# A fused low-rank update on one Trainium2 core: five loads and four stores in place of ten and eight

## The chip, the cores and the metric

The kernel runs on one core of one Trainium2 chip. The metric is device time in microseconds (us). Each time below is the median of the runs made of that kernel; the runs of one kernel lie within about one per cent of their median. A profile is taken of one of these runs and shows its span, 1.6 to 1.9 us shorter than the time. Times inside a run are counted from the start of the profile's span.

## The reference

```python
x: (16, 512, 768) float32;  A: (768, 16);  B: (16, 768);  scale = 0.5
out = x + scale * ((x @ A) @ B)
```

The 8192 rows of x and of the result are 25.2 MB each way. A and B are 48 KB each.

## The kernel before

Partition p holds 64 consecutive rows of x, so a load of n "rows" moves n x 3 KB of contiguous memory into each of 128 partitions. Everything is loaded into one buffer, changed in place, and stored from it. These are the parts that matter:

```python
LOAD_ROWS = [1, 3, 4] + [8] * 7          # rows of each load, per partition
STORE_ROWS = [8] * 8                     # rows of each store

a_f32 = const.tile([P, ND, R], fp32, name="a_f32")
nc.scalar.dma_start(out=a_f32, in_=A.rearrange("(c p) r -> p c r", p=P))     # ScalarE's queue
r = 0
for n in LOAD_ROWS:
    nc.sync.dma_start(out=x_all[:, ds(r, n), :], in_=xv[:, ds(r, n), :])     # SyncE's queue
    r += n
# [cut]
b_f32 = const.tile([R, D], fp32, name="b_f32")
nc.scalar.dma_start(out=b_f32, in_=B)
# [cut: casts of A and B to float16, the identity]

# for each step of up to 4 rows:
#   transposed(): 6 x 4 TensorE transposes of x, copied to SBUF by ScalarE
#   down():       6 matmuls with A into yt, scaled by VectorE
#   up_and_add(): for the step before: 2 matmuls with B, added to the row by VectorE
#   finished():   issues a store on SyncE's queue as soon as all of its rows are done
```

A is read with its 16-element rows spread over partitions and chunks, so its load consists of 768 pieces of 64 bytes, 48 for each of the 16 DMA engines. An x load has 128 pieces, 8 for each engine, one per partition (128 packets for each load).

## Time and profile before

| | before |
|---|---|
| time | 125.2 us |
| span of the profiled run | 123.6 us |
| x queue (q1), share of the 16 engines' span | 96.0% |
| TensorE busy | 80% |
| A landed | 4.7 us |
| last store issued / last packet written | 107.8 / 122.0 us |

The page of the kernel before, parts 1 and 2. The 40 digits are equal slices of the span, each the busy share in tenths.

```profile
PE 98.4 (80%) x614; PEld 60.9 (49%) x614; DVE 68.7 (56%) x83; ACT 52.4 (42%) x103; POOL 0.7 (1%) x6
...
PE   0569997999999999999999999999999995300000
...
DMA  4999999999999999999999999999999999999981
```

The DMA engines are full from the second slice to near the end. The queue table and the list of issues (the last column is the time from issue to landing):

```profile
q1 hardware_dynamic: 2592, 50.33, 96.0%
q10 hardware_dynamic: 816, 0.10, 0.6%
...
out_dram<-x_all SPq DMA_DIRECT2D x8, 3072.0 KB, 28.6
x_all<-in_x_dram SPq DMA_DIRECT2D x7, 3072.0 KB, 37.5
...
a_f_77<-in_A_dram ACTq DMA_DIRECT2D x1, 48.0 KB, 3.9
```

q1 is SyncE's queue with x and the result; q10 is ScalarE's, with A and B.

The kernel is bound by DMA: 25 MB in, then 25 MB out, with nothing between.

### The profile page before, as it was taken

The page shows a single profiled execution, that of the slowest core. Times are in us where ns is not written, and L with a number is a line of the kernel's source. Part 1 is how long each engine was busy: PE and PEld are TensorE (multiplying, and loading weights), DVE is VectorE, ACT ScalarE, POOL GpSimd, SP SyncE. Part 2 cuts the span into 40 slices and gives each one's busy share as a digit, 9 for nine tenths or more (in the row PEclk, how much of TensorE's full clock was granted, in tenths as well). Part 3 has the DMA queues.
Part 4 walks back from the last instruction along what each step waited for, and adds up shares of the span by engine and source line. Part 5 has one row for each costly group of instructions (what it writes and reads, how often), then busy time and mean ns, then how long its engine had stood idle before and what let it go on. Part 6 is the DMA issues. An engine that isn't in the chain of part 4 may idle for free.

```text
span 123.6 us, 1623 instructions
## 1 busy us (share of the span) xinstructions
PE 98.4 (80%) x614; PEld 60.9 (49%) x614; DVE 68.7 (56%) x83; ACT 52.4 (42%) x103; POOL 0.7 (1%) x6
## 2 busy tenths in 40 slices
PE   0569997999999999999999999999999995300000
PEld 0356472847575666666665747475656662000000
DVE  0023156666857677686868686867576688900000
ACT  4315363547373737365555546373737360000000
POOL 2000000000000000000000000000000000000000
PEclk9999999999999999999999999999999999855555
DMA  4999999999999999999999999999999999999981
GB/s 72 383 409 442 477 414 398 485 379 453 430 390 496 398 411 453 406 469 406 406 475 392 446 422 430 453 406 435 430 422 461 392 453 427 414 469 398 446 366 48
DMA packets 3416, 50.54 MB, mean 409 GB/s; under 512 B 1088, under 2 KB 1088, under 8 KB 1232
## 3 DMA queue, kind: packets, MB, share of 16 engines
q1 hardware_dynamic: 2592, 50.33, 96.0%
q10 hardware_dynamic: 816, 0.10, 0.6%
q8 instruction: 5, 0.08, 0.3%
q14 instruction: 3, 0.02, 0.0%
HBM read 25.26 MB, written 25.17 MB: 408 GB/s over the span
## 4 chain that ended last, share of the span: by engine, by line
PE 75%; DMA 5%; DVE 4%; issue 1%; DVEq 1%; SPq 0%
PE xt_ps L82 39%; PE lora_ps L108 19%; PE yt_ps L92 17%; DMA x_all<-in_x_dram 5%; DVE x_all L112 3%; DVE yt_sb L96 1%; DVEq L177 1%; SPq L60 0%
## 5 line engine op out<-in xcount | busy, mean ns | idle before, releaser
L112 DVE TENSOR_TENSOR x_all<-x_all,lora_ps 128x768 f32<-128x768 f32 x64 | 58.3, 951 | 28.7 <-PE lora_ps L108 28.7
L84 ACT CAST xt_sb<-xt_ps 128x512 f16<-128x512 f32 (+2 forms) x102 | 51.2, 568 | 47.3 <-PE xt_ps L82 47.1
L82 PE MATMUL xt_ps<-ident,x_all 128*128 128x128 f32 x384 | 52.0, 287 | 5.6 <-DMA x_all<-in_x_dram 5.6
L82 PEld LDWEIGHTS xt_ps<-ident,x_all 128*128 128x128 f32 x384 | 43.4, 145 | 17.9 <-issue 10.6
L108 PE MATMUL lora_ps<-b_mm,yt_sb 16*128 16x512 f16 (+1 forms) x128 | 27.0, 326 | 2.7 <-DVE yt_sb L96 1.6
L92 PE MATMUL yt_ps<-xt_sb,a_mm 128*16 128x512 f16 (+2 forms) x102 | 24.8, 384 | 0.0
L108 PEld LDWEIGHTS <-yt_sb 16*128 16x128 f16 x128 | 9.4, 93 | 13.8 <-issue 6.8
L92 PEld LDWEIGHTS <-a_mm 128*16 128x16 f16 x102 | 8.0, 93 | 13.6 <-issue 6.0
L96 DVE TENSOR_SCALAR yt_sb<-yt_ps 16x512 f16<-16x512 f32 (+2 forms) x17 | 10.9, 641 | 3.6 <-PE yt_ps L92 3.6
L72 DVE CAST a_mm<-a_f_77 128x96 f16<-128x96 f32 x1 | 0.2, 209 | 4.7 <-DMA a_f_77<-in_A_dram 4.7
L84 ACT ACT_TABLE_LOAD x1 | 1.3, 1283 | 1.8 <-issue 1.8
L74 DVE CAST b_mm<-b_f_89 16x768 f16<-16x768 f32 x1 | 0.5, 548 | 2.1 <-DMA b_f_89<-in_B_dram 2.1
masks.py:199 POOL TENSOR_SCALAR_AFFINE_SELECT ident<-ident 128x128 f32<-128x128 f32 x1 | 0.3, 292 | 0.1
masks.py:197 POOL MEMSET ident<- 128x128 f32 x1 | 0.2, 204 | 0.3 <-POOLq L163 0.3
L163 POOL MEMSET const-bfloat16-1.0<- 128x1 bf16 x1 | 0.1, 102 | 0.0
L163 POOL MEMSET const-uint8-127<- 128x1 uint8 x1 | 0.1, 102 | 0.0
L163 POOL MEMSET const-float32-0.0<- 128x1 f32 x1 | 0.1, 98 | 0.2 <-issue 0.2
L163 POOL MEMSET const-float32-1.0<- 128x1 f32 x1 | 0.1, 98 | 0.0
## 6 DMA issues: line engine op xcount, KB each, us to landing
out_dram<-x_all SPq DMA_DIRECT2D x8, 3072.0 KB, 28.6
x_all<-in_x_dram SPq DMA_DIRECT2D x7, 3072.0 KB, 37.5
x_all<-in_x_dram SPq DMA_DIRECT2D x1, 1536.0 KB, 10.0
x_all<-in_x_dram SPq DMA_DIRECT2D x1, 1152.0 KB, 6.7
x_all<-in_x_dram SPq DMA_DIRECT2D x1, 384.0 KB, 3.6
a_f_77<-in_A_dram ACTq DMA_DIRECT2D x1, 48.0 KB, 3.9
b_f_89<-in_B_dram ACTq DMA_DIRECT2D x1, 48.0 KB, 5.8
```

The lines of the kernel that those rows point to most:

```text
L72: nc.vector.tensor_copy(out=a_mm, in_=a_f32)
L74: nc.vector.tensor_copy(out=b_mm, in_=b_f32)
L82: nc.tensor.transpose(xt_ps[:, s, :], row(r0 + s)[:, ds(j * P, P)], ident)
L84: nc.scalar.copy(out=xt_sb[:, 0 : S * P], in_=xt_ps[:, 0:S, :])
L92: nc.tensor.matmul(yt_ps[:, 0:n], a_mm[:, j, :], xt[:, 0:n], start=(j == 0), stop=(j == ND - 1))
L96: nc.vector.tensor_scalar(out=yt_sb[:, 0:n], in0=yt_ps[:, 0:n], scalar1=sc, scalar2=None, op0=mybir.AluOpType.mult,)
L108: nc.tensor.matmul(lora_ps[:, ds(n0, n)], yt_sb[:, ds(s * P, P)], b_mm[:, ds(n0, n)], start=True, stop=True,)
L112: nc.vector.tensor_tensor(out=row(r0 + s), in0=row(r0 + s), in1=lora_ps, op=mybir.AluOpType.add)
L163: nc = _bacc.Bacc("TRN2", target_bir_lowering=False, num_devices=1)
L177: with _tile.TileContext(nc) as tc:
```

## The change

The intent: larger transfers, fewer of them, less fixed cost.

```diff
-LOAD_ROWS = [1, 3, 4] + [8] * 7
-STORE_ROWS = [8] * 8
+LOAD_ROWS = [4, 12, 16, 16, 16]
+STORE_ROWS = [20, 20, 16, 8]
```

Nothing else changes.

## The prediction

> **What bounds the kernel now.** The DMA queue. The page's queue table gives q1 96.0% of the 16 engines' span; the table of windows, 425 to 430 GB/s in every 10 to 20 us stretch from 20 to 120 us. All loads are queued ahead of the stores. TensorE heads the chain of waits (75%), but by the timeline the last store is issued at 107.84 us and lands 14.6 us later, because the store before it occupies the engines until 112.7 (first engine) to 114.8 us (last one), by its completion packets. TensorE has 4 to 6 us of slack.

> **Removed.** Per-packet cost. The DMA packet records give minima of 121 ns for 3 KB, 347 for 9 KB, 460 for 12 KB, 912 for 24 KB: 27.2 B/ns plus about 8 ns per packet. Data packets fall from 144 to 72 per engine: 72 x 8 ns = 0.58 us, and nine completion packets of 9 ns: -0.66 us. Nothing else in the 118.6 us of queue work shrinks.[...]

> **Moved.** Rows become usable later.
> - The first four rows land at about 7.8 us as before (the 3-row load released TensorE at 8.0), but the 1-row start at 4.5 us is gone.
> - Step 0 (24 transposes at the cold 213 ns, six matmuls) runs from 8.0 to 14 or 16 us. Rows 4 to 7 now come with a 12-row load; the first 16 rows land at about 18.8 us. Before, that step started at 15.05. TensorE idles 3 to 5 us.
> - That should drop the clock again. [...] The trace agrees: transposes are 213 ns apart before 15.2 us and 109 after, and the granted clock falls to 0.5 at 107.4 us after a sparse stretch. [...]
> - From the start of the rows-4-to-7 step to the last store's issue took 92.8 us; one more row of up-projection falls in it (+0.4). The last store is issued at about 18.9 + 92.8 + 0.4[...] = 114.6 us (112 without re-cooling), just past the drain of the stores ahead of it, now 112 to 114 us. Its first packet follows 1.05 us after issue (as for the first load), its eight packets per engine take 7.3 us: last packet at 123.0, against 122.06 before.

> Later loads (32 rows by 33.5 us, needed at 36) and the other stores (ready well before their turn) don't bind.

> **Prediction.** The 0.66 us gained is eaten by a late last store: 125.9 us, +0.6%. Without re-cooling 124.6; with a slow re-warm 127. Range 124.4 to 127.3. Faster by over 2%: 2%; within 2%: 90%; slower: 8%.

> **What would show it.** 1296 packets on q1; 48 KB packets near 1.81 us, 60 KB near 2.27. A TensorE wait of 3 to 5 us for a load, ending near 19 us[...]. Last store issued at 113 to 116 us, with a dip in DMA share just after 112, landing about 9 us after issue instead of 14.6.

> **What would make it wrong.** Long packets split or slower per byte; the clock staying warm (then 124.6); engines drifting further apart behind longer packets; larger first packets delaying A past 13 us.

The sum for the last store's issue came to 114.6 us; the term for re-warming is cut out of it, and the three that stand come to 112.1. The totals with re-cooling (125.9, and 127 with a slow re-warm) rest on that term, which was the author's estimate and was not shown.

## More of the kernel before

A landed 3.9 us after its issue at 0.7 us. The waits of all engines (engine, line, what it waited for: us in total, times, longest):

```profile
PE xt_ps L82 <- DMA x_all<-in_x_dram: 5.6, 2, 4.5
DVE a_mm L72 <- DMA a_f_77<-in_A_dram: 4.7, 1, 4.7
```

TensorE is held up by data for only 5.6 us, at the start.

## The result, and the profile after

| | before | after |
|---|---|---|
| time | 125.18 us | 181.68 us |
| span | 123.6 | 179.8 |
| x queue, share of the engines' span | 96.0% | 65.4% |
| A landed | 4.7 us | 62.5 us |
| last store issued | 107.8 us | 164.1 us |

The ratio is 1.451, 95% interval 1.446 to 1.457. A ratio here is the mean time of one kernel's fast runs over that of the other's fast runs of the same rounds, so it is not quite the ratio of the medians quoted.

The same parts of the page after the change:

```profile
PE 99.2 (55%) x608; PEld 62.2 (35%) x608; DVE 68.4 (38%) x82; ACT 51.8 (29%) x97; POOL 0.7 (0%) x6
...
PE   0440000000000095999899999999999999961000
...
DMA  6999898989898400000000599950099990898892
```

TensorE does the same work, but stands still for eleven slices, about 50 us. The DMA engines stand still as well, later: the loads are through at slice 14, and no row is ready to be stored until slice 23. The queue table and issues:

```profile
q1 hardware_dynamic: 1296, 50.33, 65.4%
q10 hardware_dynamic: 816, 0.10, 0.4%
...
a_f_77<-in_A_dram ACTq DMA_DIRECT2D x1, 48.0 KB, 61.7
b_f_84<-in_B_dram ACTq DMA_DIRECT2D x1, 48.0 KB, 61.4
```

The x queue itself did what was hoped: half the packets, and 65.4% of 179.8 us is 117.6 us of work against 118.7 before. But A, 48 KB, took 61.7 us to land instead of 3.9. The waits:

```profile
DVE a_mm L72 <- DMA a_f_77<-in_A_dram: 62.5, 1, 62.5
PEld L92 <- DVE a_mm L72: 52.3, 1, 52.3
PE yt_ps L92 <- DVE a_mm L72: 51.9, 1, 51.9
...
PE xt_ps L82 <- DMA x_all<-in_x_dram: 7.1, 1, 7.1
```

Read this as a chain: VectorE's cast of A waits for A's DMA until 62.5 us, and the first matmul that uses A (L92) waits 51.9 us for that cast. x itself was waited for only once, for the first load. The chain of waits on the page names this stretch "another core or an unknown queue 34%"; the list of waits is the view that names A.

The table of windows shows what the delay costs the DMA queue (columns: window, length, busy time of TensorE's matmuls, its weight loads, VectorE, ScalarE and GpSimd with counts, granted clock, DMA share, GB/s). First two windows of the kernel before, then three of the changed one:

```profile
15.00:60.00 45.00, 44.23 (x293) 28.14 (x292) 31.08 (x37) 24.11 (x47) 0.00 (x0) 1.00 1.00 429
65.00:100.00 35.00, 35.00 (x232) 21.89 (x231) 25.48 (x32) 18.76 (x36) 0.00 (x0) 1.00 1.00 429
```

```profile
15.00:60.00 45.00, 0.00 (x0) 0.00 (x0) 0.00 (x0) 0.00 (x0) 0.00 (x0) 1.00 1.01 433
65.00:100.00 35.00, 32.34 (x192) 20.10 (x192) 20.02 (x24) 16.32 (x31) 0.00 (x0) 0.95 0.00 1
120.00:130.00 10.00, 10.00 (x64) 5.86 (x62) 7.60 (x9) 5.43 (x11) 0.00 (x0) 1.00 0.01 2
```

Before, both work all the time. After, from 15 to 60 us only DMA works, from 65 to 100 us only the compute engines. Two stages that overlapped now follow each other. The third line is the wait for the second 20-row store.

Why was A late? The trace records each DMA packet with its queue, size and time. Each load and store of x also leaves 16 packets of 4 bytes (288 for 18 transfers before, 144 for nine after), which start as its data packets end; they are the completion packets, read here as one per engine. Counting the data packets that start in each 0.2 us (this is a tabulation of those records, not a view of the page):

```
            x packets started      A packets started
before
3.3 us      23 of 3 KB              58
3.5          4 of 3 KB, 1 of 9 KB  300
3.7          1 of 3 KB, 7 of 9 KB  308
3.9          9 of 9 KB              82
4.1         11 of 9 KB              20
after
4.1          5 of 12 KB              5
4.3          9 of 12 KB              9
4.5          5 of 12 KB              5
7.5          8 of 36 KB              8
7.7          6 of 36 KB              6
7.9          2 of 36 KB              2
```

In these counts after the change, one 64-byte piece of A passes for each x packet, whether that packet is 12 or 36 KB. Over the whole load phase 41 of A's 48 pieces per engine passed, beside 37 x packets (the few extra pieces passed where one x load ended and the next began); the last seven went when the x queue was empty. In the kernel before, A's pieces ran almost alone: the single-row first load was nearly over when they arrived at 3.35 us, and no packet of the second load started before 3.70 us.

### The profile page after: what moved, and what is told of

Its sections match the earlier page's. It is cut to its first block, busy times and chain, and to the rows that moved or that the text cites. A ratio compares the mean times of both kernels' runs of the same rounds, so it can differ in the third digit from the quotient of the medians.

```text
span 179.8 us, 1574 instructions
## 1 busy us (share of the span) xinstructions
PE 99.2 (55%) x608; PEld 62.2 (35%) x608; DVE 68.4 (38%) x82; ACT 51.8 (29%) x97; POOL 0.7 (0%) x6
## 3 DMA queue, kind: packets, MB, share of 16 engines
q1 hardware_dynamic: 1296, 50.33, 65.4%
## 4 chain that ended last, share of the span: by engine, by line
PE 50%; another core or an unknown queue 34%; DVE 5%; issue 1%; DVEq 0%
PE xt_ps L82 26%; PE lora_ps L108 12%; PE yt_ps L92 12%; DVE x_all L112 4%; DVE yt_sb L96 1%; DVEq L177 0%; DVE a_mm L72 0%
## 5 line engine op out<-in xcount | busy, mean ns | idle before, releaser
L84 ACT CAST xt_sb<-xt_ps 128x512 f16<-128x512 f32 x96 | 50.5, 594 | 104.2 <-PE xt_ps L82 104.2
L82 PE MATMUL xt_ps<-ident,x_all 128*128 128x128 f32 x384 | 52.9, 293 | 7.1 <-DMA x_all<-in_x_dram 7.1
L92 PE MATMUL yt_ps<-xt_sb,a_mm 128*16 128x512 f16 x96 | 24.8, 395 | 51.9 <-DVE a_mm L72 51.9
L82 PEld LDWEIGHTS xt_ps<-ident,x_all 128*128 128x128 f32 x384 | 45.2, 150 | 18.2 <-issue 12.3
L92 PEld LDWEIGHTS <-a_mm 128*16 128x16 f16 x96 | 7.5, 91 | 65.7 <-DVE a_mm L72 52.3
L108 PE MATMUL lora_ps<-b_mm,yt_sb 16*128 16x512 f16 (+1 forms) x128 | 26.5, 323 | 4.6 <-DVE yt_sb L96 2.3
L72 DVE CAST a_mm<-a_f_77 128x96 f16<-128x96 f32 x1 | 0.2, 211 | 62.5 <-DMA a_f_77<-in_A_dram 62.5
L96 DVE TENSOR_SCALAR yt_sb<-yt_ps 16x512 f16<-16x512 f32 x16 | 10.8, 673 | 9.0 <-PE yt_ps L92 9.0
## 6 DMA issues: line engine op xcount, KB each, us to landing
a_f_77<-in_A_dram ACTq DMA_DIRECT2D x1, 48.0 KB, 61.7
```

The lines of the kernel that those rows point to most:

```text
L72: nc.vector.tensor_copy(out=a_mm, in_=a_f32)
L82: nc.tensor.transpose(xt_ps[:, s, :], row(r0 + s)[:, ds(j * P, P)], ident)
L84: nc.scalar.copy(out=xt_sb[:, 0 : S * P], in_=xt_ps[:, 0:S, :])
L92: nc.tensor.matmul(yt_ps[:, 0:n], a_mm[:, j, :], xt[:, 0:n], start=(j == 0), stop=(j == ND - 1))
L96: nc.vector.tensor_scalar(out=yt_sb[:, 0:n], in0=yt_ps[:, 0:n], scalar1=sc, scalar2=None, op0=mybir.AluOpType.mult,)
L108: nc.tensor.matmul(lora_ps[:, ds(n0, n)], yt_sb[:, ds(s * P, P)], b_mm[:, ds(n0, n)], start=True, stop=True,)
```

## The experiments

### 1 and 2. One half of the change at a time

```diff
 # loads_only                                   # stores_only
-LOAD_ROWS = [1, 3, 4] + [8] * 7                 LOAD_ROWS = [1, 3, 4] + [8] * 7
+LOAD_ROWS = [4, 12, 16, 16, 16]                -STORE_ROWS = [8] * 8
 STORE_ROWS = [8] * 8                           +STORE_ROWS = [20, 20, 16, 8]
```

Loads only:

> Theory (A's 768 small descriptors wait one x packet each behind the long loads, and the loads alone do this): A lands near 62 us as after the change; the last store is issued near 164 us and, as the 8-row store before it has long landed, lands 8.7 us later: span 174, time 175 to 177 us. Rival (the large stores cause the loss): about 125 us.

Measured: 175.98 us, A landed at 62.4 us. Stores only:

> Theory: A lands near 4.6 us as before; 32 data packets of 8 ns and four completion packets fewer on each engine: 124.9 us, ratio 0.997. Rival (the large stores cause the loss): well above 130 us.

Measured: 125.84 us, ratio 1.0039 with an interval of 1.0000 to 1.0078, so the expected small gain did not come. The loads alone cost 50.8 us (175.98 - 125.14). The large stores cost at most a per cent by themselves, and another 5.7 us on top of the late A (181.68 - 175.98).

### 3 and 4. Give A its way past the loads

`short_first` keeps the large loads but brings back the single-row first load:

```diff
-LOAD_ROWS = [4, 12, 16, 16, 16]
+LOAD_ROWS = [1, 3, 12, 16, 16, 16]
```

> Loads of 1, 3, 12, 16, 16, 16 rows, large stores, A where it was. Theory (A passes in the dry spell of the x queue right after a short first load; the packet size of the later loads does not matter to it): A lands near 4.6 us, TensorE starts near 4.5 us, waits for the 12-row load until about 18.7 us; 124.6 to 126.5 us. Rival (large x packets as such keep A back): A lands after 30 us or later, 150 us or more.

Measured: 130.41 us; VectorE waited for A until 5.2 us. `a_behind_first` keeps the change's rows and moves A and B to the x queue:

```diff
 for n in LOAD_ROWS:
     nc.sync.dma_start(out=x_all[:, ds(r, n), :], in_=xv[:, ds(r, n), :])
+    if r == 0:
+        nc.sync.dma_start(out=a_f32, in_=A.rearrange("(c p) r -> p c r", p=P))
+        nc.sync.dma_start(out=b_f32, in_=B)
     r += n
-nc.scalar.dma_start(...)     # [shortened: A's and B's own loads from ScalarE go]
```

> The changed kernel with A and B issued on the x loads' own queue, right behind the first load. Theory (turn-taking between two queues is the cause): A lands near 8 us, no wait for it; what is left is what was predicted for the change: TensorE idle for 3 us or more until about 19 us, cold transposes after it, last store issued at 112 to 116 us, 124.5 to 127 us. Rival (A's many small descriptors are slow in themselves behind large packets, whatever the queue): A late again, 150 us or more.

Measured: 129.49 us. The issues of this kernel:

```profile
a_f<-in_A_dram SPq DMA_DIRECT2D x1, 48.0 KB, 6.3
b_f<-in_B_dram SPq DMA_DIRECT2D x1, 48.0 KB, 6.2
```

On the x queue A landed 6.3 us after its issue, with the same 768 pieces and the same large packets behind it, against 61.7 us on ScalarE's queue. This removes 52.2 us of the 56.5 us and rules out the rival that small pieces are slow in themselves. The rest of the expectation was missed in both runs: 129.5 and 130.4 us lie above their ranges. About 4 us were still unexplained; runs 10 and 11 take that up.

This run also tests the clock part of the prediction. The windows of `a_behind_first`:

```profile
12.90:19.70 6.80, 4.21 (x24) 2.09 (x23) 4.23 (x5) 1.01 (x3) 0.00 (x0) 1.00 1.02 441
19.70:23.10 3.40, 3.40 (x18) 3.07 (x17) 0.00 (x0) 2.52 (x5) 0.00 (x0) 0.51 0.80 347
```

TensorE ran only eight matmuls between 14.3 us and 18.6 us, when the 12-row load landed, and the granted clock then fell to 0.51 for 3.4 us. The prediction expected the clock to drop after TensorE had been idle for 3 to 5 us. This trace shows the drop, but no such idle stretch before it: TensorE's longest pause in that stretch was 0.78 us. In `short_first` the half clock lasted twice as long, from 17.95 to 24.78 us. The last store was issued at 111.7 us, against a predicted 114.6 (112 without re-cooling).

### 5. A first load of two rows

```diff
-LOAD_ROWS = [4, 12, 16, 16, 16]
+LOAD_ROWS = [2, 2, 12, 16, 16, 16]
```

> Loads of 2, 2, 12, 16, 16, 16 rows, large stores. Theory (what counts is whether the x queue runs dry when A's descriptors arrive at about 3.3 us, and the second load's packets are ready by about 4 us): the first load lasts until about 4.4 us, so there is no dry spell and A takes turns with 6 KB, 36 KB and 48 KB packets: it lands near 60 us, about 180 us. Rival (the second load is held back until A is through): A lands below 8 us, about 125 us. In between if some engines are dry.

Measured: 130.19 us, A landed at 6.1 us. The theory, as stated, missed. The packet records show a dry spell again: between 4.2 and 5.0 us, 699 of A's 768 pieces passed, and the second load's first packets started only from 4.55 us on, although SyncE had issued that load at 1.2 us. So an issued load is not yet a load with packets: here 3.3 us lay between the two, with most of A passing meanwhile.

### 6. Small packets, long first load

```diff
 # the kernel before, with
-LOAD_ROWS = [1, 3, 4] + [8] * 7
+LOAD_ROWS = [4, 4] + [8] * 7
```

> The kernel before with loads of 4, 4 and seven of 8 rows: packets of at most 24 KB. Theory (one 64-byte descriptor of A for each x packet, whatever its size, as soon as the first load outlasts A's arrival): A's 48 turns per engine last until about 39 us, when the first 40 rows are through; the seventh load waits for A's semaphore; the last store is issued near 141 us, 149 to 155 us in all. Rival (packets above 24 KB are needed for the loss): A lands near 5 us, 125 us.

Measured: 147.89 us (ratio 1.18). VectorE waited for A until 38.4 us, as computed from 48 turns:

```profile
DVE a_mm L72 <- DMA a_f<-in_A_dram: 38.4, 1, 38.4
```

No packet in this kernel is above 24 KB. The sizes the kernel had always used are enough to do the damage once the first load is four rows. The total fell 1 us below the expected range. It also holds a wait that the change's five loads do not have: as expected, the seventh load waited for A's semaphore, 34.5 us.

### 7 and 8. Other ways to bring A

`a_8_packets` loads A as 128 pieces of 384 bytes, 8 per engine, and takes the features in the matching order:

```diff
-nc.scalar.dma_start(out=a_f32, in_=A.rearrange("(c p) r -> p c r", p=P))
+nc.scalar.dma_start(out=a_f32, in_=A.rearrange("(p c) r -> p c r", c=ND))
-nc.tensor.transpose(xt_ps[:, s, :], row(r0 + s)[:, ds(j * P, P)], ident)
+nc.tensor.transpose(xt_ps[:, s, :], row(r0 + s)[:, ds(j, P, step=ND)], ident)
```

> The changed kernel with A loaded as 128 descriptors of 384 bytes (8 for each engine instead of 48), the feature order of the transposes changed to match. Theory (one turn per descriptor): A lands after 8 turns, four of 0.46 us and four or five of 1.37 us, so near 12 us, before the matmuls that need it are much delayed: 125 to 128 us. Rival (the second queue is starved as such until the x queue is empty): A near 61 us, about 180 us.

Measured: A landed at 7.4 us, earlier than the 12 us expected: by the packet records its pieces arrived already at 2.60 us (3.77 in the changed kernel) and passed mostly beside 12 KB packets:

```profile
DVE a_mm L72 <- DMA a_f<-in_A_dram: 7.4, 1, 7.4
```

The time was 139.17 us, well above the range. The strided reads came with a price of their own. The group of transposes' weight loads in this kernel, then in `a_behind_first`:

```profile
L82 PEld LDWEIGHTS xt_ps<-ident,x_all 128*128 128x128 f32 x384 | 57.6, 236 | 18.4 <-issue 8.0 <-PE yt_ps L92 5.6 <-ACT xt_sb L84 4.1
```

```profile
L83 PEld LDWEIGHTS xt_ps<-ident,x_all 128*128 128x128 f32 x384 | 45.0, 149 | 19.0 <-issue 12.0 <-PE yt_ps L93 5.6 <-DMA x_all<-in_x_dram 1.1
```

The mean went from 149 to 236 ns. That this makes up the whole excess was not tested. So the theory is borne out for A's landing, and the total says nothing about it.

`a_gpsimd` issues A from GpSimd:

```diff
-nc.scalar.dma_start(out=a_f32, in_=A.rearrange("(c p) r -> p c r", p=P))
+nc.gpsimd.dma_start(out=a_f32, in_=A.rearrange("(c p) r -> p c r", p=P))
```

> The changed kernel with A issued from GpSimd. If turns are one descriptor each for any queue: A lands near 61 us again, about 181 us. If the software queue's turns hold several descriptors: A lands before 15 us, 125 to 128 us.

Measured: 132.40 us, A landed at 10.3 us. The queue table of this run:

```profile
q1 hardware_dynamic: 1296, 50.33, 90.9%
...
q0 software_dynamic: 32, 0.05, 0.1%
```

The software queue shows 32 packets for A: by the records one of 3072 bytes per engine, which is 48 pieces of 64 bytes, and one for completion. The same 48 pieces passed as one packet there and as 48 on ScalarE's queue, and A landed at 10.3 us against 62.5. The total lies above the expected range. As in runs 3 and 4 the 16-row store came late: it was issued at 104.0 us, and by the completion packets the engines had drained at 99.8 to 101.7.

### 9. Half as many pieces

```diff
-nc.scalar.dma_start(out=a_f32, in_=A.rearrange("(c p) r -> p c r", p=P))
+nc.scalar.dma_start(
+    out=a_f32.rearrange("p (c t) r -> p c (t r)", t=2),
+    in_=A.rearrange("(c p t) r -> p c (t r)", p=P, t=2),
+)
-nc.tensor.transpose(xt_ps[:, s, :], row(r0 + s)[:, ds(j * P, P)], ident)
+nc.tensor.transpose(xt_ps[:, s, :], row(r0 + s)[:, ds((j // 2) * 2 * P + j % 2, P, step=2)], ident)
```

> The changed kernel with A loaded as 384 descriptors of 128 bytes, 24 for each engine instead of 48, feature order matched. Theory (one turn per descriptor): 6 turns of 0.46 us during the first load, 8 of 1.37 us, the last 9 or 10 of 1.82 us: A lands at 33 us, plus or minus 2 (61.6 us with 48, 7.4 us with 8). Total 148 to 160 us, depending on how fast TensorE reads the strided rows. Rival (A waits for the end of the x queue): 62 us.

Measured: 156.86 us, and A at 33.0 us:

```profile
DVE a_mm L75 <- DMA a_f<-in_A_dram: 33.0, 1, 33.0
```

The landing time follows the number of pieces: 8 gave 7.4 us, 24 gave 33.0, 48 gave 62.5. The rival that a second queue is starved outright predicts 62 us for all three and falls.

### 10 and 11. Where the last 4 us went

In `a_behind_first` the windows show an empty DMA stretch late in the run:

```profile
96.00:98.00 2.00, 2.00 (x16) 1.38 (x15) 0.91 (x2) 1.41 (x3) 0.00 (x0) 1.00 0.64 276
98.00:102.00 4.00, 4.00 (x28) 2.44 (x27) 3.32 (x5) 1.90 (x4) 0.00 (x0) 1.00 0.15 61
102.00:104.00 2.00, 2.00 (x17) 1.37 (x15) 1.09 (x2) 1.35 (x4) 0.00 (x0) 1.00 1.55 664
```

The two 20-row stores were through at 98.0 us on the first engine and 100.2 us on the last, but the 16-row store can be issued only when its last row is done, at 101.2 us. (In `short_first` it was issued at 102.9 us, after a drain at 98.7 to 101.1.) `behind_stores8` goes back to eight stores and changes nothing else:

```diff
-STORE_ROWS = [20, 20, 16, 8]
+STORE_ROWS = [8] * 8
```

> Loads of 4, 12, 16, 16, 16 rows with A and B behind the first load on the x queue, and eight stores of 8 rows. Theory (what was left of the loss in that kernel is the 16-row store, which was issued at 101.2 us when the engines had drained at 98.0 to 100.3): every store is now issued before its turn, no empty DMA stretch; 124.7 to 125.6 us. Rival (the loss comes from the late last store after the clock dropped, as the prediction had it): 127 us or more.

Measured: 125.21 us, ratio to the kernel before 0.9996 (0.9962 to 1.0029). The same windows:

```profile
96.00:98.00 2.00, 2.00 (x17) 1.38 (x15) 0.87 (x1) 1.45 (x3) 0.00 (x0) 1.00 0.97 418
98.00:102.00 4.00, 4.00 (x29) 2.44 (x27) 3.36 (x5) 1.87 (x4) 0.00 (x0) 1.00 1.03 442
102.00:104.00 2.00, 2.00 (x17) 1.37 (x16) 1.06 (x2) 1.35 (x4) 0.00 (x0) 1.00 1.00 430
```

Compute is the same to a few hundredths of a microsecond, and the last store is issued at 111.7 us in both, yet the empty stretch is gone and with it 4.3 us. The late last store, which the prediction feared, costs nothing: it is issued before the seventh store has drained (112.6 to 114.9 us by the completion packets). The half clock is in this kernel too, from 18.7 to 22.1 us.

`mixed_sizes` tries to keep the good of both, with A where it was:

```diff
-LOAD_ROWS = [1, 3, 4] + [8] * 7
+LOAD_ROWS = [1, 3, 4, 8, 8, 8, 16, 16]
-STORE_ROWS = [8] * 8
+STORE_ROWS = [16, 16, 16, 8, 8]
```

> Loads of 1, 3, 4, 8, 8, 8, 16, 16 rows and stores of 16, 16, 16, 8, 8: long packets only where nothing waits for them. A lands near 4.6 us, no empty DMA stretch; 40 data packets fewer on each engine, 0.3 to 0.4 us less: 124.8 us, ratio 0.997. If the per-packet saving is not real: 125.2 us or above.

Measured: 125.53 us, ratio 1.0003 (0.9967 to 1.0039): no gain. By the expectation's own test (125.2 us or above) the saving is not shown. The packet records give 118.15 us of work per engine on the x queue against 118.63. But `a_gpsimd`, with the same x packets as the change, has 118.23 against its 117.64, so a difference of half a microsecond can have other causes. A 16-row store was again issued (at 90.7 us) just after the first engine had drained (90.4 us). No version here beats the kernel before by a measurable amount.

### 12 and 13. What keeps the second load back

`a_issued_later` is the kernel before, with its single-row first load and its eight-row stores. Only A is issued later, because ScalarE first writes a few bytes of A's tile:

```diff
+late = const.tile([P, 8], fp32, name="late")
+nc.vector.memset(late, 0.0)
+nc.scalar.copy(out=a_f32[:, 0, 0:8], in_=late)
 nc.scalar.dma_start(out=a_f32, in_=A.rearrange("(c p) r -> p c r", p=P))
```

> The kernel before, row counts unchanged, but ScalarE first writes a few bytes of A's tile, so that A is issued at about 3.3 us, after the first five x loads, instead of at 0.8 us. Theory (A passed alone in the kernel before because its descriptors were produced before those of the second load, which came late enough for the short first load to have drained): now the second load's packets are ready first, there is no dry spell, A takes one turn for each x packet until the first six loads (32 rows) are through and lands near 32 us; about 143 us in all. Rival (a short first load or packets of at most 24 KB suffice, whatever the order of issue): A lands near 7 us, 125 to 126 us.

Measured: 155.01 us. A was issued at 2.70 us, after five x loads. The second load's packets now started from about 3.0 us (3.70 before), there was no dry spell, and A took its turns from 6.5 us to 43.5 us:

```profile
a_f<-in_A_dram ACTq DMA_DIRECT2D x1, 48.0 KB, 42.1
```

The landing, at 44.8 us, was later than the 32 us computed because the seventh load waited for B's semaphore rather than for A's, so x packets kept coming; only the tenth waited for A's. The direction is settled: the row counts of the kernel before do not protect A by themselves; issued at 0.7 us, before the second load, it landed at 4.7 us, and issued at 2.70 us, after it, at 44.8. The records show when packets start; that descriptors were produced earlier or later is not shown. Nor is the earlier issue enough by itself: in the changed kernel, too, A was issued (0.73 us) before the second load (1.16 us).

`three_row_first` lies between the two-row and the four-row first load:

```diff
-LOAD_ROWS = [4, 12, 16, 16, 16]
+LOAD_ROWS = [3, 1, 12, 16, 16, 16]
```

> Loads of 3, 1, 12, 16, 16, 16 rows, large stores. In the two-row run A passed alone at 4.3 to 5.0 us and the second load's first packets started at 4.6 to 5.0 us; with a four-row first load there was no dry spell at 6.2 us. Theory (the second load's packets exist from a fixed moment, near 4.7 us, when A's have been produced): the first load now lasts until about 5.2 us, so there is no dry spell, A takes turns and lands near 61 us, 180 us or more. Rival (each first load up to three rows leaves a dry spell because the second load is made ready only when the first drains): A lands below 8 us, about 130 us.

Measured: 179.71 us, VectorE waited for A until 58.3 us, both a little under what was expected:

```profile
DVE a_mm L72 <- DMA a_f<-in_A_dram: 58.3, 1, 58.3
```

There was no dry spell: the first load ended at 5.1 to 5.6 us, and the second load's packets followed at once. One row more in the first load, 3 KB per partition, is worth 50 us. The "fixed moment" of this theory can't be right in that form, though, because in the kernel before the second load's packets began at 3.70 us and in the two-row run only from 4.55 us. In both, the first of them started within 0.01 us of the first of A's completion packets (3.69 and 4.54 us), that is, when one engine was through with its 48 pieces; about half of all pieces had started by then. In the three-row run they came, from 5.12 us on, long before any engine was through with A (35.8 us at the earliest), so being through with A is not the condition either. That the packets of the second load wait for something that A's load, issued ahead of them, has to do first would fit these start times. It is a guess: what they wait for, no run shows.

## Why the prediction was wrong

- **"Removed": -0.66 us.** Right in mechanism and about right in size. 48 KB packets took 1813 ns at least (1.81 predicted) and 60 KB packets 2267 (2.27). Counted with the shortest packet of each size, the x queue's work falls by 0.8 us per engine, 117.02 to 116.22. The sums of all packets, 118.63 and 117.64, differ by 1.0, but such sums move by 0.6 us between runs with the same x packets (`a_gpsimd`: 118.23). The gain does not reach the time.
- **The step that failed.** "Step 0 (24 transposes at the cold 213 ns, six matmuls) runs from 8.0 to 14 or 16 us." That takes A as landed, as before. It was listed last among the things that would make it wrong ("larger first packets delaying A past 13 us") and never costed, although the trace held the packet counts that ask the question: 48 pieces per engine beside 8 x packets per load. A landed at 62.5 us, so the six matmuls of step 0 began only at 62.7 us. Moving A to the x queue takes 52.2 of the 56.5 us away.
- **The second failed step: "the other stores (ready well before their turn) don't bind".** The 16-row store was not ready. In `a_behind_first`, the kernel that comes closest to what was predicted, it was issued at 101.2 us after the engines had drained at 98.0 to 100.2. That is 4.3 us, shown by going back to eight stores. A store of n rows is issued when its last row is done; the prediction compared its issue with its turn only for the last store.
- **Idle TensorE, half clock.** Half right: in `a_behind_first` 0.51 was granted from 19.7 to 23.1 us, after a sparse stretch and not an idle one of 3 to 5 us. It costs nothing in the end: `behind_stores8` has the same half clock, and its total is that of the kernel before (0.9996). The profile's clock row does not show the slow start: in the kernel before it reads as full up to its first record at 15.2 us, while the transposes started mostly 213 ns apart until then and 109 ns apart after.
- **The DMA bound.** Right for before, and the reason why nothing gained was visible: with A early and the stores on time, 125.21 us.

## What to carry to other kernels

Before making the packets of a busy queue larger or its first transfer longer, count the pieces of each small load on another queue: on the two hardware queues here 41 of A's 48 pieces per engine passed beside 37 x packets, and the late A cost about 50 us on top of 125. Put what the first matmul needs into the same queue, behind the first data that it works on (A landed 6.3 us after its issue there), rather than trust to a gap. Size a store by when its last row is done against when the stores ahead of it are through; one store too large left the engines empty for about 4 us.
